# ConvFFN of a hybrid MLA/GLA layer on one core: the prompt's output gate folded into w_down, sums begun from the residual rows, gate and conv rows loaded at other places

## The chip, the cores and the metric

The kernel runs on one core of a Trainium2 chip. The metric is the device time of one launch in microseconds, as the median of several runs; less is better. The engines are named as the profile names them: PE (TensorE; PEld is its weight load), DVE (VectorE), ACT (ScalarE), POOL (GpSimd) and SP (SyncE, the queue that issues every transfer of this kernel).

## What is computed

One layer of a streaming encoder for a prompt of 2048 tokens and a sample of 64 tokens, all in float32, with 1024 model columns. The first half (projections, attention, gated linear attention) isn't touched by the change. The second half is, per sequence:

```
x  = x + mods[2][:, None, :] * mixed              # residual rows, the first gate
h  = _modulate(x, p['g_norm2'], mods[3], mods[4])
a, g = jnp.split(h @ p['w_up'], 2, axis=-1)       # 1024 -> 2 x 2816
a_ext = concat([hist, a]);  conv = b_conv + sum_j w_conv[j] * a_ext[:, j:j+L]    # width 3
f  = (gelu(conv) * g) @ p['w_down']               # 2816 -> 1024
y  = x + mods[5][:, None, :] * f                  # the second gate: one value per column and sequence
```

The last line can be written, for one sequence, as `y = x + u @ (w_down * gate)`, because the gate depends on the output column alone.

## The kernel before

**Products.** Every large product is made of three float32r products of a high and a low part: a `split` makes the high part on ACT (a cast) and the low part (source minus high part) on DVE or POOL. w_up is applied with a Strassen-like scheme of seven products of blocks (`PRODUCTS`), so each step also has block sums (POOL, line 1205), weight splits (ACT line 1456, DVE and POOL line 1398) and recombinations.

**Projection stage** (lines 1069 to 1137 and 1229 to 1254). `out_tile` is a generator, run for 17 tiles of tokens (16 of the prompt, one of the sample) with the steps load, mT, proj, res, norm and done interleaved by hand in the loop of line 1230. It multiplies by w_out, applies the first gate (line 1093), adds x and stores the residual rows in DRAM (`x1_d`, line 1096), normalises, and writes blocks for the up-projection: those of pass 0 stay on the chip (`h2`), those of the later passes go to DRAM (`comb_d`, lines 1134 to 1136). The gate row comes by `gate_rows` (line 1178), a broadcast to all partitions, once for the prompt (t = 0) and once for the sample (t = 16), into one buffer (`gate`, bufs=1 in that tag). `conv_rows` (line 1212) loads w_conv, b_conv and the sample's history as rows into the buffers `xn` and `comb`, which every tile also uses, and transposes them on PE to columns; it is called at t = 3.

**ConvFFN** (from line 1257). Three passes over the 22 blocks of 128 FFN columns, 66 steps: pass 0 and pass 1 have 6 tiles of the prompt each, pass 2 has the last 4 and the sample. Pass 1 goes through the blocks backwards, so the w_down rows of the last step of a pass serve the first step of the next (`wd_kept`). The function `slot(n, ...)` writes down the instructions of step n as events with times: `base` is the step's start, `end[m]` the end of product m, `after` the end of the step. The events are sorted by these times, and PE, ACT, DVE and POOL execute them in that order; only the transfers on SP are placed by the framework's own scheduler. In a step PE does products 1, 6, 2, 5, then down tiles (`"d"`) of the step before between products 3, 7, 4 and behind them:

```
seq = [1, 6, 2, 5, "d", 3, "d", 7, "d", 4] + ["d"] * 8
```

A down tile (`down_tile`, line 1485) is six matmuls into two PSUM banks (line 1496), and an addition of the two halves to the tile's sum `acc` on DVE (line 1507); in the first step of a pass the sum begins with a copy on ACT (line 1505). `rows` loads 128 rows of w_down (`sd`, line 1188), `rows_hi` and `lo` split them (ACT line 1433, DVE line 1398). In the last step of a pass each finished sum gets, in halves of 512 columns, a multiplication by the gate on DVE (`gate_`, line 1543), an addition of the residual rows on POOL (`finish_`, line 1548; the rows come as `xs`, line 1534, in two buffers) and a store (line 1549). For passes 0 and 1 these events are spread over the next step and a half by `late`; in pass 2 they follow the sums at once. The last step also fetches the inputs of the next pass (`fetch`, line 1480, 14 transfers of 768 KB). Eight `acc` buffers go round; three lie in the pool `ac0`, five in `ac1`, which is opened in place of the projection stage's `wk4b`. `conv_state` (line 1568) stores the convolution's last rows in the last step: two transposes, two copies on DVE to `ob`, two stores; `ob` takes the two buffers of `xs`.

Of the kernel before, what the change touches and what calls it, by code (L numbers as in the profile page):

```python
# [11 lines left out]
F32 = mybir.dt.float32  # L12
# [9 lines left out]
P = 128  # L22
# [39 lines left out]
def kernel(  # L62
# [1006 lines left out]
    def out_tile(t, n, seq, src, pos0, tok0):  # L1069
# [2 lines left out]
        yield "load"  # L1072
        wk = wk4
        if t in (0, NT):
            gt[seq] = gate_rows(wk, 0, seq, "gate")
        x = wk4b.tile([P, D], F32, tag="x", name="x", bufs=2)
        Q.dma_start(x[:n], src)
        mT = [wk.tile([P, KD, P], F32R, tag=f"mT{i}", name=f"mT{i}", bufs=2) for i in range(2)]
# [102 lines left out]

    c7 = ctx.enter_context(ExitStack())
    fw = None
    g2 = []

    def load_rows(f):
        s = fw.tile([P, D], F32, tag="fst", name="fst", bufs=4)
# [24 lines left out]
    def conv_rows(pool):  # L1212
        fr = pool.tile([4 * NF, P], F32, tag="xn", name="fr")
        Q.dma_start(fr[:3 * NF], w_conv.rearrange("j (f p) -> (j f) p", p=P))
        Q.dma_start(fr[3 * NF:], b_conv.rearrange("j (f p) -> (j f) p", p=P))
        fh = pool.tile([4 * NF, P], F32, tag="comb", name="fh")
        Q.dma_start(fh[:2 * NF], state_ffn_conv.rearrange("j (f p) -> (j f) p", p=P))
        for src, dst, n in ((fr, fcol, 4 * NF), (fh, hist, 2 * NF)):
            pt = bank()
            T.transpose(pt[:, :n], src[:n], ident[:n, :n])  # L1220
            V.tensor_copy(dst.rearrange("p j f -> p (j f)"), pt[:, :n])

    c6, c6a = ctx.enter_context(ExitStack()), ctx.enter_context(ExitStack())
    wk4b = c6.enter_context(tc.tile_pool(name="wk4b", bufs=1, side="right", reuse_waits="tile"))
# [1 line left out]

    next(outs[0])
    for t in range(len(tiles) - 1):  # L1230
        g, nxt = outs[t], outs[t + 1]
        last = t == len(tiles) - 2
        next(nxt)
        next(g)
        if t == 3:
            conv_rows(wk4b)
        if last:
            next(outs[t - 1])
            next(outs[t - 1])
            next(nxt)  # L1240
            next(nxt)
            project(t, t + 1, ks=range(3))
            next(outs[t - 1])
            project(t, t + 1, ks=range(3, KD))
        else:
            project(t)
            if t:
                next(outs[t - 1])
                next(outs[t - 1])
            next(nxt)  # L1250
            if t:
                next(outs[t - 1])
# [13 lines left out]
    with ExitStack() as c8:  # L1266
# [8 lines left out]
        def acc_tile():  # L1275

            nonlocal n_acc
            i, n_acc = n_acc % 8, n_acc + 1
            return ac[i > 2].tile([P, D], F32, tag=f"acc{i}", name="acc")

        halo = wk.tile([P, NF, 2], F32, tag="halo", name="halo")
        cout = [wk.tile([P, 2, NF], F32, tag=f"cout{s}", name=f"cout{s}") for s in range(2)]

# [21 lines left out]
        def slot(n, base, w, raw, raw_next, behind):  # L1305
# [121 lines left out]
            def rows():  # L1427
                o["sd"] = load_rows(f)

            def rows_hi():  # L1430
                nonlocal wd_kept
                o["wd"] = wd_kept = two("wd", (P, D))
                S.copy(o["wd"][0], o["sd"])  # L1433
# [1 line left out]
            def rows_kept():  # L1435
                o["wd"] = wd_kept

            if first_f and n:
                at(base + 2, rows_kept)
            else:  # L1440
                at(base + 2, rows)
                at(after + 1.0, rows_hi)
                at(after + 2.5, lambda: lo(o["wd"], o["sd"], V))

# [40 lines left out]
            def down_tile(i, t):  # L1485

                rows_ = P if i < nt else SMP
                c0 = i * P if i < nt else nt * P + 2

                def products():  # L1490
                    if first_f:
                        acc[i] = acc_tile()
                    o["po", i] = po = [bank(), bank()]
                    for a, b in ((0, 0), (0, 1), (1, 0)):
                        for c in range(2):
                            T.matmul(po[c][:rows_], o["u"][a][:, c0:c0 + rows_],  # L1496
                                     o["wd"][b][:, c * 512:(c + 1) * 512], start=a + b == 0, stop=a == 1)

                def add():
                    o["acc", i] = acc[i]  # L1500
                    for c in range(2):
                        cc = slice(c * 512, (c + 1) * 512)
                        x, y = acc[i][:rows_, cc], o["po", i][c][:rows_]
                        if first_f:
                            S.copy(x, y)
                        else:
                            V.tensor_tensor(x, x, y, op=ALU.add)  # L1507

                if n == 0 and i == 3:
                    at(t - .01, open_acc)  # L1510
                at(t, products)
                t += 6 * .232
                at(t + .1, add)
                if last_f:
                    tile_ = t0 + i if i < nt else NT
                    last = n + 1 == len(steps)
                    late = o.setdefault("late", t) + 5.5 * i + 1.6

                    def gate_load():
                        if i in (0, nt) and (n + 1 == NF or i == nt):  # L1520
                            if i == nt:
                                g2[:] = [acc_tile()]
                            else:
                                g2[:] = [ac[1].tile([P, D], F32, tag="gate", name="gate")]
                            Q.dma_start(g2[0], gate_d[1, int(i == nt):int(i == nt) + 1].partition_broadcast(P))
                        o["gate", i] = g2[0]

                    def residual(c):
                        if c == 0 or not last:
                            gate_load()  # L1530
                        src = x1_d[tile_ * P:tile_ * P + rows_]
                        if not last:
                            o["xs", i, c] = x = ac[1].tile([P, 512], F32, tag="xs", name="xs", bufs=2)
                            Q.dma_start(x[:rows_], src[:, c * 512:(c + 1) * 512])
                        elif c == 0:
                            x = fw.tile([P, D], F32, tag="fst", name="fst", bufs=4) if i < 3 else acc_tile()
                            Q.dma_start(x[:rows_], src)
                            o["xs", i, 0], o["xs", i, 1] = x[:, :512], x[:, 512:]

                    def gate_(c):  # L1540
                        cc = slice(c * 512, (c + 1) * 512)
# [3 lines left out]
                    def finish_(c):  # L1545
                        cc = slice(c * 512, (c + 1) * 512)
                        a = o["acc", i][:rows_, cc]
                        (V if last and i == nt and c else G).tensor_tensor(a, a, o["xs", i, c][:rows_], op=ALU.add)  # L1548
                        Q.dma_start((y_sample if i == nt else y_prompt[tile_ * P:tile_ * P + rows_])[:, cc], a)

                    for c in range(2):
                        at(base + 8.0 + i if last else late - 4 + c, residual, c)
                        at(t + 1.4 + c * .1 if last else late + 2.5 * c, gate_, c)
                        at(t + 1.5 + c * .1 if last else late + 1 + 2.5 * c, finish_, c)
                return t

            return after, w_next, [lambda t, i=i: down_tile(i, t) for i in range(nt + smp)]
# [10 lines left out]
        def conv_state():  # L1568
            for s, dst in ((0, conv_prompt), (1, conv_sample)):
                pt = bank()  # L1570
                T.transpose(pt[:2 * NF, :P], cout[s].rearrange("p j f -> p (j f)"), ident)
                ob = ac[1].tile([P, 512], F32, tag="xs", name="ob", bufs=2)
                V.tensor_copy(ob[:2 * NF, :P], pt[:2 * NF, :P])
                Q.dma_start(dst.rearrange("j (f p) -> (j f) p", p=P), ob[:2 * NF, :P])

# [78 lines left out]
```

## Time and profile before

| | us |
|---|---|
| median of 3 runs | 3186.03 (3184.51 to 3191.58) |
| the profiled execution | 3196.8 |
| its span, first to last instruction | 3195.0 |
| PE busy, DVE busy, POOL busy in the span | 3037.7, 2471.9, 1438.8 |
| the projection stage | about 1446 to 1683 |
| ConvFFN, pass 0, pass 1, pass 2 begin | 1683, 2232, 2751 |

Times in the views are microseconds from the span's start, durations of single instructions nanoseconds where "mean" or "median" is said. "PE bank L1326 x48" in the chain is a run of 48 matmuls of line 1326. A bracket at the end of a timeline row is the idle time of the engine before it and what ended it. A row of the table by stretches gives the stretch, its length, the busy time of PE, PEld, DVE, ACT and POOL with the number of instructions of each, PE's granted clock as a share of full speed, the busy share of the DMA engines and the GB/s moved. An "SPq" row is an issue of a transfer.

### The profile page before, as it was taken

Reading aid. Unit: us, or ns where it says so; the run is one execution under the profiler, and the core shown is the slowest. Engines: PE = TensorE matmul, PEld = TensorE weight load, DVE = VectorE, ACT = ScalarE, POOL = GpSimd, SP = SyncE. Lnnn points to the kernel's source line nnn. Section 1 sums busy time; section 2 is a strip of 40 time slices with the busy share of each in tenths; the row PEclk is TensorE's granted clock in tenths of the full one; section 3 lists DMA queues with packets and bytes.
Section 4 is the critical chain, followed back from the end, with each engine's and each line's share of the span. In section 5 each row is a group of like instructions: output and inputs, shape, how many; then the busy total and the mean of one; then the engine's idle time right before and its main releaser. Section 6 shows DMA issues by size and latency. Waiting matters only on the chain.

```text
span 3195.0 us, 46983 instructions
## 1 busy us (share of the span) xinstructions
PE 3037.7 (95%) x16730; PEld 2662.0 (83%) x16730; DVE 2471.9 (77%) x4642; ACT 1497.6 (47%) x3254; POOL 1438.8 (45%) x1194
## 2 busy tenths in 40 slices
PE   7999899999989999998995999999999999999997
PEld 4999788788758888886874999999899999889996
DVE  4776678778688888874564778777878787899998
ACT  4655433333257777773544443433444343344442
POOL 0223222212132222201446666664866666688885
PEclk9999899999979999999997999999999999999999
DMA  7554521111121112103474222224421212532322
GB/s 255 158 132 122 151 70 60 53 50 53 37 82 51 50 48 64 38 28 110 161 235 141 72 73 67 71 68 168 156 72 60 80 60 75 201 116 82 97 80 83
DMA packets 186778, 306.09 MB, mean 96 GB/s; under 512 B 59959, under 2 KB 112775, under 8 KB 186543
## 3 DMA queue, kind: packets, MB, share of 16 engines
q1 hardware_dynamic: 186543, 303.09, 30.2%
q8 instruction: 132, 2.16, 0.3%
q14 instruction: 103, 0.84, 0.1%
HBM read 227.79 MB, written 75.24 MB: 95 GB/s over the span
## 4 chain that ended last, share of the span: by engine, by line
PE 48%; POOL 4%; DVE 2%; DMA 2%; issue 1%; ACT 1%; POOLq 0%; DVEq 0%; SPq 0%
PE bank L1326 27%; PE bank L1496 15%; PE bank L96 3%; DMA comb_d<-comb 1%; PE bank L882 1%; PE bank L869 1%; POOL sraw L1205 1%; POOL comb L91 1%; DVE acc L1543 1%; DVE acc L1507 1%; POOL acc L1548 0%; ACT comb L1117 0%; POOL wu L1398 0%; PE bank L841 0%; PE bank L843 0%
## 5 line engine op out<-in xcount | busy, mean ns | idle before, releaser
L1326 PE MATMUL bank<-h,wu 128*128 128x384 f32 (+1 forms) x5544 | 958.1, 328 | 41.5 <-ACT m L1345 23.3
L1326 PEld LDWEIGHTS bank<-h,wu 128*128 128x128 f32 x5544 | 923.5, 190 | 71.4 <-ACT m L1345 27.5
L1496 PE MATMUL bank<-wd,u 128*128 128x512 f32 (+1 forms) x2244 | 567.7, 396 | 3.0 <-ACT wd L1433 1.4
L1398 POOL TENSOR_TENSOR wu<-sraw,wu 128x512 fp32r<-128x512 f32 x252 | 364.0, 1444 | 367.4 <-ACT wu L1456 367.2
L1507 DVE TENSOR_TENSOR acc<-acc,bank 128x512 f32<-128x512 f32 (+1 forms) x714 | 450.8, 678 | 48.5 <-PE bank L1496 45.5
L1496 PEld LDWEIGHTS bank<-wd,u 128*128 128x128 f32 (+1 forms) x2244 | 410.0, 186 | 87.4 <-ACT wd L1433 1.9
L96 PE MATMUL bank<-w_g,hs 128*128 128x512 f32 (+4 forms) x1632 | 319.6, 347 | 0.0
L1398 DVE TENSOR_TENSOR wu<-fst,wu 128x512 fp32r<-128x512 f32 x189 | 212.2, 1148 | 102.5 <-ACT wu L1456 100.9
L96 PEld LDWEIGHTS bank<-w_g,hs 128*128 128x128 f32 (+1 forms) x1632 | 249.8, 188 | 33.4 <-issue 2.7
L91 DVE TENSOR_TENSOR pp<-bank,pp 128x512 fp32r<-128x512 f32 (+5 forms) x344 | 196.2, 577 | 40.5 <-ACT pp L88 36.1
L882 PE MATMUL bank<-pp,vv 128*128 128x512 f32 (+5 forms) x688 | 210.8, 393 | 13.0 <-DVE ob L906 6.7
L857 ACT ACTIVATE pr<-bank,mx 128x512 f32<-128x512 f32 (+4 forms) x328 | 204.7, 629 | 30.6 <-DVE mx L850 21.1
L1384 DVE SCALAR_TENSOR_TENSOR cv<-a_sb,fcol,cv 128x768 f32<-128x768 f32 (+1 forms) x132 | 215.7, 1634 | 4.1 <-ACT cv L1380 1.8
L88 ACT CAST pp<-bank 128x512 fp32r<-128x512 f32 (+5 forms) x344 | 170.0, 504 | 103.5 <-PE bank L869 101.4
L845 DVE TENSOR_REDUCE mx<-bank 128x1 f32<-128x512 f32 (+4 forms) x328 | 195.0, 599 | 24.8 <-PE bank L844 18.8
L1351 POOL TENSOR_TENSOR m<-m,m 128x384 f32<-128x384 f32 (+1 forms) x132 | 172.8, 1309 | 72.9 <-ACT m L1345 66.8
L96 PE MATMUL bank<-w_o,mT 128*128 128x512 f32 (+1 forms) x816 | 199.1, 402 | 0.2 <-ACT mT L88 0.2
L1456 ACT CAST wu<-sraw 128x512 fp32r<-128x512 f32 x252 | 154.9, 615 | 78.5 <-PE bank L1326 49.0
L869 PE MATMUL bank<-ident,pr 128*128 128x128 f32 (+1 forms) x1112 | 181.0, 278 | 3.2 <-DVE pp L91 2.3
L1205 POOL TENSOR_TENSOR sraw<-fst 128x512 f32<-128x512 f32 x128 | 178.2, 1393 | 11.6 <-DMA fst<-w_up 11.6
L96 PEld LDWEIGHTS bank<-w_o,mT 128*128 128x128 f32 (+1 forms) x816 | 151.1, 188 | 38.9 <-ACT mT L88 0.5
L1345 ACT COPY m<-bank 128x384 f32<-128x384 f32 (+1 forms) x198 | 89.7, 453 | 172.1 <-PE bank L1326 170.9
(260 smaller groups left out, 5224.2 us busy)
## 6 DMA issues: line engine op xcount, KB each, us to landing
fst<-w_up SPq DMA_DIRECT2D x128, 512.0 KB
fst<-w_down SPq DMA_DIRECT2D x64, 512.0 KB
x<-x_prompt SPq DMA_DIRECT2D x32, 512.0 KB
ada_w<-w_ada SPq DMA_DIRECT2D x64, 256.0 KB
h<-comb_d SPq DMA_DIRECT2D x14, 768.0 KB
comb_d<-hi SPq DMA_DIRECT2D x10, 896.0 KB
wst<-w_ada SPq DMA_DIRECT2D x16, 512.0 KB
hT_d<-hT SPq DMA_DIRECT2D x16, 512.0 KB
```

Of the source, the lines that this page charges most:

```text
L91: (lo_eng or V).tensor_tensor(lo, src, hi.bitcast(F32), op=ALU.subtract)
L96: T.matmul(out, a, b, start=first and i == 0, stop=last and i == 2)
L845: V.reduce_max(mx[:qn, c:c + 1], po[:qn, :b - a], axis=AX.X)
L857: S.activation(pr[:qn, :b - a], box["s", i, j][:qn, :b - a], AF.Exp, bias=nb, accum_out=ls[:qn, i, j:j + 1])
L869: T.transpose(pt[:kn, i * qn:(i + 1) * qn], pr[:qn, j * P - a:j * P - a + kn], ident[:qn, :qn])
L882: T.matmul(box["o"][:, cs_], vv[:kn, key0 // P + j, :], pp[i][:kn, cs_], start=j == 0 and i == 0, stop=j == nk - 1 and i == 1)
L1205: G.tensor_tensor(s, x, y, op=op)
L1326: T.matmul(b, w[m][i][:, k], hv[j][:, :, k], start=first and k + i + j == 0, stop=k == 3 and i == 1, skip_group_check=not first)
L1384: V.scalar_tensor_tensor(v, o["a"][:, j:j + tot], col(j), v, op0=ALU.mult, op1=ALU.add)
L1398: eng.tensor_tensor(out[1], src, out[0].bitcast(F32), op=ALU.subtract)
L1496: T.matmul(po[c][:rows_], o["u"][a][:, c0:c0 + rows_], o["wd"][b][:, c * 512:(c + 1) * 512], start=a + b == 0, stop=a == 1)
L1507: V.tensor_tensor(x, x, y, op=ALU.add)
```

## The change

Four things. (a) In passes 0 and 1 each block of w_down rows is multiplied by the prompt's gate (`rows_gated`, 128 x 1024 on DVE, 43 times: not in step 22, which keeps the rows of step 21); step 44, the first of pass 2, loads its rows anew, without the gate. (b) In these passes the sum's buffer is loaded with the residual rows (`open_sum`) and every step adds to it on DVE; the finished sum is stored as it is, in one transfer. (c) The second gate's row is loaded once before the steps (`gate2`), so that two `acc` buffers remain in `ac0`; `ob` has a buffer of its own, one for both uses; the first gate of the sample goes into a buffer of `mx`. (d) `conv_rows` is a generator: its loads stand before the projection loop, its transposes behind the first tile's product.

```diff
         if t in (0, NT):
-            gt[seq] = gate_rows(wk, 0, seq, "gate")
+            gt[seq] = gate_rows(wk, 0, seq, "gate") if t == 0 else gate_rows(w3, 0, seq, "mx", 2)
...
         Q.dma_start(fh[:2 * NF], state_ffn_conv.rearrange("j (f p) -> (j f) p", p=P))
+        yield
         for src, dst, n in ((fr, fcol, 4 * NF), (fh, hist, 2 * NF)):
             pt = bank()
             T.transpose(pt[:, :n], src[:n], ident[:n, :n])
             V.tensor_copy(dst.rearrange("p j f -> p (j f)"), pt[:, :n])
+        yield
...
+    conv = conv_rows(wk4b)
+    next(conv)
     next(outs[0])
     for t in range(len(tiles) - 1):
...
-        if t == 3:
-            conv_rows(wk4b)
...
             project(t)
-            if t:
+            if t == 0:
+                next(conv)
+            else:
                 next(outs[t - 1])
                 next(outs[t - 1])
...
-            return ac[i > 2].tile([P, D], F32, tag=f"acc{i}", name="acc")
+            return ac[i > 1].tile([P, D], F32, tag=f"acc{i}", name="acc")
+
+        gate2 = gate_rows(wk, 1, 0, "gate2")
...
+            def rows_gated():
+                V.tensor_tensor(o["sd"], o["sd"], gate2, op=ALU.mult)
...
-            if first_f and n:
+            if n == NF:
                 at(base + 2, rows_kept)
             else:
                 at(base + 2, rows)
+                if p + 1 < len(PASSES):
+                    at(end[2] + .7, rows_gated)
                 at(after + 1.0, rows_hi)
                 at(after + 2.5, lambda: lo(o["wd"], o["sd"], V))
...
+                folded = p + 1 < len(PASSES)
+
+                def open_sum():
+                    acc[i] = acc_tile()
+                    if folded:
+                        Q.dma_start(acc[i], x1_d[(t0 + i) * P:(t0 + i + 1) * P])
+
                 def products():
-                    if first_f:
-                        acc[i] = acc_tile()
                     o["po", i] = po = [bank(), bank()]
...
-                        if first_f:
+                        if first_f and not folded:
                             S.copy(x, y)
                         else:
                             V.tensor_tensor(x, x, y, op=ALU.add)
 
-                if n == 0 and i == 3:
-                    at(t - .01, open_acc)
+                if first_f:
+                    if n == 0 and i == 0:
+                        at(27.5, open_acc)
+                    at(max(28.0 + .2 * i, t - 5.0) if folded else t, open_sum)
                 at(t, products)
...
-                if last_f:
...
+                if last_f and folded:
+                    at(t + 1.8, lambda: Q.dma_start(y_prompt[tile_ * P:tile_ * P + rows_], acc[i][:rows_]))
+                elif last_f:
 
                     def gate_load():
...
+                        o["gate", i] = gate2
+                        if i == nt:
+                            o["gate", i] = acc_tile()
+                            Q.dma_start(o["gate", i], gate_d[1, 1:2].partition_broadcast(P))
...
-                        at(base + 8.0 + i if last else late - 4 + c, residual, c)
-                        at(t + 1.4 + c * .1 if last else late + 2.5 * c, gate_, c)
-                        at(t + 1.5 + c * .1 if last else late + 1 + 2.5 * c, finish_, c)
+                        at(t + 1.4 + c * .1, gate_, c)
+                        at(t + 1.5 + c * .1, finish_, c)
...
-                ob = ac[1].tile([P, 512], F32, tag="xs", name="ob", bufs=2)
+                ob = ac[1].tile([P, P], F32, tag="ob", name="ob")
```

## Rows read from the trace of the kernel before

**Rows 1.** The page's first line.
```profile
span 3195.0 us, 46983 instructions
```

**Rows 2.** The table by stretches: two projections, a step of pass 1, two steps of pass 2.
```profile
1496.93:1510.60 13.67, 13.67 (x51) 10.87 (x51) 0.88 (x2) 0.00 (x0) 0.00 (x0) 0.82 0.00 0
...
1525.34:1536.58 11.24, 11.24 (x50) 9.01 (x50) 5.57 (x12) 6.24 (x14) 6.07 (x8) 1.00 0.24 93
...
2770.44:2821.23 50.79, 41.69 (x230) 36.34 (x230) 46.41 (x55) 20.82 (x42) 49.18 (x36) 0.90 0.53 171
2379.67:2402.87 23.20, 23.20 (x122) 21.57 (x121) 18.53 (x26) 9.32 (x16) 14.35 (x12) 1.00 0.24 69
```

**Rows 3.** The chain that ended last, in the ConvFFN: start, us, what.
```profile
2231.72 8.45 PE bank L1326 x48
...
2310.10 8.45 PE bank L1326 x48
...
2821.23 6.47 PE bank L1326 x48
...
2839.51 6.46 PE bank L1326 x48
```

**Rows 4.** Timeline of PE around the transposes of the conv rows.
```profile
1487.20 0.27 PE L1220 MATMUL bank<-ident,fr 88*128 88x88 f32 x1 [1.94 <-DMA fr<-b_conv]
1496.60 0.33 PE L1220 MATMUL bank<-ident,fh 44*128 44x44 f32 x1 [9.13 <-DMA fh<-state_ffn_conv]
```

**Rows 5.** Waits of the SP queue, 1672 to 1690: for whom, us in total, times, longest.
```profile
SPq L1178 <- DVE bank L1093: 10.6, 1, 10.6
```

**Rows 6.** Timeline of SP: the issue of the last three of four first w_up loads.
```profile
1688.15 3.85 SPq L1193 DMA_DIRECT2D fst<-w_up  x3
```

**Rows 7.** Timeline of POOL at the start of pass 0.
```profile
1695.73 1.26 POOL L1205 TENSOR_TENSOR sraw<-fst 128x512 f32<-128x512 f32 x1 [11.64 <-DMA fst<-w_up]
```

**Rows 8.** Instructions of lines 1543 and 1548: min/median/max ns, first and last start.
```profile
L1543 DVE TENSOR_TENSOR acc<-acc,gate x32: 673/1320/1784, 2242.6 to 3185.4; 128x512 f32<-128x512 f32 x32
...
L1548 POOL TENSOR_TENSOR acc<-acc,xs x24: 1285/1708/2005, 2243.3 to 2807.1; 128x512 f32<-128x512 f32 x24
```

**Rows 9.** Groups of DVE by form in 17 steps of pass 1: busy, mean ns, idle before.
```profile
L1398 DVE TENSOR_TENSOR wd<-fst,wd 128x1024 fp32r<-128x1024 f32 x17 | 20.8, 1221 | 0.0
```

**Rows 10.** Timeline of DVE: one busy moment behind pass 0, then a step of pass 1.
```profile
2289.34 2.30 DVE L1398 TENSOR_TENSOR wd<-fst,wd 128x1024 fp32r<-128x1024 f32 x1
...
2363.88 1.78 DVE L1398 TENSOR_TENSOR wu<-fst,wu 128x512 fp32r<-128x512 f32 x1 [2.46 <-ACT wu L1456]
2366.13 1.28 DVE L1507 TENSOR_TENSOR acc<-acc,bank 128x512 f32<-128x512 f32 x2 [0.47 <-PE bank L1496]
2368.53 0.56 DVE L1368 TENSOR_TENSOR a_sb<-m,bank 128x384 f32<-128x384 f32 x1 [1.11 <-issue]
...
2369.65 1.29 DVE L1507 TENSOR_TENSOR acc<-acc,bank 128x512 f32<-128x512 f32 x2 [0.35 <-PE bank L1496]
...
2375.66 0.54 DVE L1348 TENSOR_TENSOR m<-m,bank 128x384 f32<-128x384 f32 x1
```

**Rows 11.** Timeline of SP in the same step.
```profile
2359.68 0.33 SPq L1188 DMA_DIRECT2D fst<-w_down  x1
```

**Rows 12.** The transfer view, 2359 to 2369 in 40 slices: GB/s moved in each.
```profile
GB/s 0 0 0 0 0 0 131 131 98 229 197 393 410 311 213 279 229 344 426 262 279 131 131 0 0 0 0 0 0 0 98 262 213 246 197 360 426 180 115 0
```

**Rows 13.** Timeline of PE: three down tiles at the end of that step.
```profile
2375.30 4.38 PE L1496 MATMUL bank<-wd,u 128*128 128x512 f32 x18
```

**Rows 14.** The chain, 1474 to 1541: a small load from its issue to its landing.
```profile
1485.66 1.41 DMA fr<-b_conv
```

**Rows 15.** Timeline of DVE in the last step.
```profile
3164.17 0.48 DVE L1573 COPY ob<-bank 44x128 f32<-44x128 f32 x2 [1.33 <-PE bank L1571]
...
3170.62 1.21 DVE L1398 TENSOR_TENSOR wd<-fst,wd 128x1024 fp32r<-128x1024 f32 x1
```

**Rows 16.** Timeline of PE: the last down tiles.
```profile
3171.88 6.81 PE L1496 MATMUL bank<-wd,u 128*128 128x512 f32 x28 [1.12 <-DVE wd L1398]
```

More of the change, by code (lines that the diff above doesn't have):

```diff
@@ L1183 @@
     fw = None
-    g2 = []
     def load_rows(f):
@@ L1513, in down_tile, with residual @@
                 at(t + .1, add)
-                if last_f:
-                    tile_ = t0 + i if i < nt else NT
-                    last = n + 1 == len(steps)
-                    late = o.setdefault("late", t) + 5.5 * i + 1.6
+                tile_ = t0 + i if i < nt else NT
+                if last_f and folded:
+                    at(t + 1.8, lambda: Q.dma_start(y_prompt[tile_ * P:tile_ * P + rows_], acc[i][:rows_]))
+                elif last_f:
                     def gate_load():
[L1520 to L1538, printed above, removed]
+                        o["gate", i] = gate2
+                        if i == nt:
+                            o["gate", i] = acc_tile()
+                            Q.dma_start(o["gate", i], gate_d[1, 1:2].partition_broadcast(P))
+                    def residual():
+                        gate_load()
+                        x = o["xs", i] = fw.tile([P, D], F32, tag="fst", name="fst", bufs=4) if i < 3 else acc_tile()
+                        Q.dma_start(x[:rows_], x1_d[tile_ * P:tile_ * P + rows_])
                     def gate_(c):
@@ L1547, in finish_ @@
                         a = o["acc", i][:rows_, cc]
-                        (V if last and i == nt and c else G).tensor_tensor(a, a, o["xs", i, c][:rows_], op=ALU.add)
+                        (V if i == nt and c else G).tensor_tensor(a, a, o["xs", i][:rows_, cc], op=ALU.add)
                         Q.dma_start((y_sample if i == nt else y_prompt[tile_ * P:tile_ * P + rows_])[:, cc], a)
+                    at(base + 8.0 + i, residual)
                     for c in range(2):
-                        at(base + 8.0 + i if last else late - 4 + c, residual, c)
-                        at(t + 1.4 + c * .1 if last else late + 2.5 * c, gate_, c)
-                        at(t + 1.5 + c * .1 if last else late + 1 + 2.5 * c, finish_, c)
+                        at(t + 1.4 + c * .1, gate_, c)
+                        at(t + 1.5 + c * .1, finish_, c)
                 return t
@@ L1571, in conv_state @@
                 T.transpose(pt[:2 * NF, :P], cout[s].rearrange("p j f -> p (j f)"), ident)
-                ob = ac[1].tile([P, 512], F32, tag="xs", name="ob", bufs=2)
+                ob = ac[1].tile([P, P], F32, tag="ob", name="ob", bufs=2)
                 V.tensor_copy(ob[:2 * NF, :P], pt[:2 * NF, :P])
```

## Prediction

> **What bounds the kernel now.** The profiled execution took 3196.8 us with a span of 3195.0 [rows 1]; the sum below is made against it, and the median of the runs, 3186.0, is 10.8 us less, so I take differences alone over to the median. First I read the table by stretches. A step of passes 0 and 1 takes 23.20 us, and PE is busy for all of it; DVE works 18.53 us of it, POOL 14.35 [rows 2]. In steady steps PE is the bound, and nothing that this change moves between DVE, ACT and POOL can shorten one. It can win only where PE waits, and lose where it makes PE wait. So I went through the chain for places in which the steps are not regular, and found four that the diff touches.
>
> The first is the conv rows in the projection stage: PE idles 1.94 and then 9.13 us for their loads [rows 4], and the 48 matmuls behind take 13.67 us at a granted clock of 0.82 (between 1.2 and 2.4 GHz), where the same work takes 11.24 at 1.00 later [rows 2]. The second is the start of pass 0: SP stands 10.6 us behind one load, the sample's first gate, which needs the buffer that DVE's last multiplication of the prompt reads [rows 5]; w_up loads wait behind it until 1688.15 [rows 6], and POOL starves 11.64 us for them [rows 7]. The third and fourth are the two pass boundaries. The three steps from 2231.72 to 2310.10 [rows 3] take 78.38 us; three regular ones would take 69.60, so 8.8 are lost. Behind pass 1, 50.79 us pass where two regular steps stand [rows 2], 36.56 by the period of 18.28 in pass 2 [rows 3], so 14.2 are lost. In the latter stretch POOL is busy 49.18 of 50.79 us and DVE 46.41 [rows 2]: the gate's multiplications (median 1.32 us, up to 1.78) and the residual additions (median 1.71) [rows 8] hold up the recombinations that free PE's banks.
>
> **The parts and their price.**
>
> *Conv rows.* The loads are issued ahead of the first tile's product (48 matmuls, 11.24 us [rows 2]) and the transposes stand behind it, where 1.41 us is what one load takes [rows 14]. The two transposes (0.27 and 0.33 us [rows 4]) and two small copies stay, at another tile. Gone are 1.94 + 9.13 = 11.1 us of idle PE, and 13.67 - 11.24 = 2.4 of slow clock: 13.5. Low end 11.1, if the clock is still recovering from something else. On SP three small issues, some 0.33 us each [rows 11], pass the first tile's gate and x, which are read behind that product too. The buffers `xn` and `comb` are free of conv rows before the first tile's norm needs them. The stage behind is bound by PE too, so the gain is not taken back.
>
> *The sample's gate.* Its buffer is free as soon as tile 15 is transposed, so the wait of 10.6 us goes. What is late next on SP: the stores of tile 14's blocks and of tile 15's residual rows, which stand in front of three of the four w_up loads and wait for DVE's work on the same tiles. If the scheduler leaves them there, the loads come earlier by the gate's own issue, about 1.3 us (three took 3.85 [rows 6]); if it puts the loads ahead, POOL's 11.6 us [rows 7] go. The order on SP isn't written in the code. I take the lower, 1.3, since nothing but the gate is taken out of the order, and keep 0 and 11.6 as ends.
>
> *The multiplications into w_down.* 43 of 128 x 1024. The nearest row is the subtraction of the same shape on DVE, 1.22 us [rows 9], 2.30 with POOL at work beside it [rows 10]: 52 to 99 us of DVE in all. DVE idles 23.20 - 18.53 = 4.7 us a step, so there is room, but the multiplication has its place: behind the addition of product 6, at 2361.42 in the step shown (the 2.46 us of idle ahead of 2363.88 [rows 10]). Its rows are issued at 2359.68 [rows 11]; with the w_up rows behind them they land between 2362.8 (half of the 1.05 MB moved) and 2364.9 (all of it) [rows 12]. It ends between 2362.8 + 1.22 = 2364.0 and 2364.9 + 2.30 = 2367.2. Queued behind it is the split of product 2's block, 0.69 to 1.78 us, which ended at 2365.66; at worst it ends at 2369.0, 3.3 us late. Behind that come idle times of 0.47, 1.11 and 0.35 us [rows 10], which take up 1.9: DVE goes into the taps at most 1.4 us late. Who waits for DVE there is PE's last down tile, which needs the bank that the addition at 2375.66 (+0.54 = 2376.20) frees [rows 10] and starts at 2375.30 + 2 x 1.40 = 2378.1 [rows 13]: 1.9 us of slack. Price: nothing at either end, by 0.5 us at the worse one. POOL has 8.8 us of idle a step.
>
> *The boundary behind pass 0.* Gone: 12 gate multiplications (12 x 1.32 = 16 us of DVE), 12 additions (12 x 1.71 = 21 us of POOL), 12 half loads with two buffers on SP, 12 copies on ACT. Added: 12 additions on DVE at about 0.64 [rows 10], 8 us, as in any step, and 6 loads of whole residual tiles. The boundary steps then hold a regular step's work, and I take all of the 8.8 us. Low end 0: the loads wait for the stores of the buffers that they reuse, and SP stands still in front of w_up. The loads of the next pass's inputs aren't the cause now, since PE ran the step from 2231.72 without a pause, so they need not become one.
>
> *The boundary behind pass 1.* The same 12 and 12 go, nothing comes on DVE but one more split of w_down rows (1.22 to 2.30 us), with a cast on ACT and a load in step 44. Of 14.2 us I take 13, low end 5 (a third).
>
> *The start of pass 0* has the 12 additions in place of copies on ACT, and six loads. The sums for the tiles 2 to 5 lie where the projection's last tile is stored from, so these loads wait for that store, and the first additions for them. Price 0, for a whole step of PE's work lies between; at worst one load's landing, 2.6 us (half of 5.2 for two [rows 11, 12]).
>
> *The last step.* `ob` has one buffer for two uses: DVE's second copy now waits for the first store, where both took 0.48 us together [rows 15]. Behind it stand the second tap, the last split of w_down (3170.62 [rows 15]) for which PE's last matmuls wait [rows 16], and then DVE's own additions and gates to the end. A small transfer takes 1.41 us [rows 14], with 0.33 for the issue [rows 11] 1.7 us, and all of it is on the path. The ends are 0, if something else on DVE has to wait as long there, and 5.2, which two loads of 512 KB took [rows 11, 12]. The Trainium skill (DMA: Bandwidth & Descriptors, "Anatomy of one DMA") gives about 2.0 us as the fixed cost of a transfer, on another issuing path; with it this term would be 2.3 and the sum 0.6 smaller. The trace has 1.41 for a load and no store of this kind with somebody waiting.
>
> Sum: 13.5 + 1.3 + 8.8 + 13 - 1.7 = 34.9 us less: 3186.0 - 34.9 = 3151. The lows make 11.1 + 0 + 0 + 5 - 2.6 - 5.2 = 8 (3178), the highs 13.5 + 11.6 + 8.8 + 14.2 = 48 (3138).
>
> **The rivals.**
>
> *The w_up loads come 10 us earlier.* For it: they need only memory that the projection's weights leave, and the first of the four was issued before the gate. Against it: the other three were not ahead of the stores in the order before. Time: 3151 - 10 = 3141. 14%.
>
> *The boundaries keep their pauses.* SP is in order, and a load of residual rows into a buffer whose store hasn't landed stops w_up and w_down behind it; before, SP waited there too, for POOL, and PE's waits were put down to ACT and POOL. If half of the 21.8 us stay and the start loses a little: about 3165 to 3170. 14%.
>
> *Slower: the multiplication stops DVE, and DVE stops PE, in each of 43 steps.* It is the only new wait of a regular step: a load's landing now stands in the middle of DVE's queue, where before nobody read it until the next step. For it: 0.5 us between my worst case and the slack. Against it: DVE's 4.7 us of idle. It cancels the rest at 34.9 / 43 = 0.81 us a step, and is slower by 0.2% (6.4 us) at 0.96; for that the rows would have to land at about 2366.4 or later with POOL beside the multiplication, some 6.7 us behind the issue. At 1.1 us a step: 3198. 6% for that, and 6% for the stretch between, where nothing can be told from no change. The skill (SBUF: State Buffer, "Who interferes with whom") says that DVE with two SBUF inputs and a reading POOL instruction exclude each other for a whole instruction; the trace agrees in kind, 1.22 against 2.30, and it would hold POOL back as well, which speaks for this rival.
>
> **How the numbers follow.** The forecast has 60%: 3151, with its own range from 3146 to 3160. Early loads 14% (3141), kept pauses 14% (3168), cancelled 6% (3180 to 3192), slower 6%. About 0.2% is what a measurement of this kernel can tell from no change: its three runs lie 7 us apart. Faster 0.88, same 0.06, slower 0.06. The range from 3139 to 3173 leaves out the last two cases and a little of each side.
>
> **What would show it.** PE without idle at line 1220 and 48 matmuls in 11.2 us behind; steps of 23.2 us in passes 0 and 1, with the multiplication ending before 2367 in a step that begins as the one shown; both boundaries within 2 us of regular steps, no lines 1543 and 1548 there; about 1.5 us between the two copies to `ob`. It is wrong if a regular step is longer than 23.3 us, if PE waits at the boundaries for banks or w_up still, or if the start of pass 0 changes by more than 5 us.

## The result, and the profile after

| | before | after |
|---|---|---|
| median of 4 runs, us | 3185.27 (3183.45 to 3191.58) | 3151.76 (3147.85 to 3157.83) |
| ratio after / before | | 0.9891, 95% interval 0.9873 to 0.9908 |
| profiled execution, us | 3196.8 | 3147.85 |
| its span, us | 3195.0 | 3146.0 |
| from TensorE's first projection product to the end of the span, us | 1748.1 | 1713.95 |

The change makes the kernel 33.5 us faster. The two spans differ by 49.0 us, but 14.8 of that lie ahead of the first projection product, where the two programs are the same: executions of one program differ there by several us (the changed kernel's first projection begins at 1432.05 in this trace and at 1437.25 in that of after_again below). So traces are compared below by the last row of the table, from that product on, or by shorter stretches.

**The conv rows.** Timeline of PE (start, us, engine, line, operation, tiles; in brackets the idle time before it), against [rows 4]:

```profile
1432.05 11.51 PE L96 MATMUL bank<-w_o,mT 128*128 128x512 f32 x48 [0.24 <-ACT mT L88]
1443.40 0.24 PE L1220 MATMUL bank<-ident,fr 88*128 88x88 f32 x1
1443.57 0.26 PE L1220 MATMUL bank<-ident,fh 44*128 44x44 f32 x1
...
1630.38 9.77 PE L96 MATMUL bank<-w_o,mT 128*128 128x512 f32 x40 [1.16 <-DVE x L1094]
...
1640.77 13.26 PE L96 MATMUL bank<-w_o,mT 128*128 128x512 f32 x56
...
1678.00 8.90 PE L1331 MATMUL bank<-h,wu 128*128 128x384 f32 x34 [4.04 <-POOL wu L91]
1690.15 6.04 PE L1331 MATMUL bank<-h,wu 128*128 128x384 f32 x24 [3.25 <-ACT m L1350]
...
1720.85 6.28 PE L1331 MATMUL bank<-h,wu 128*128 128x384 f32 x24 [4.25 <-ACT m L1350]
```

The same view of the kernel before: the first and the last product of the stage, and the 24 products at which the opening below ends.

```profile
1446.89 1.19 PE L96 MATMUL bank<-w_o,mT 128*128 128x512 f32 x4 [0.24 <-ACT mT L88]
...
1667.46 13.70 PE L96 MATMUL bank<-w_o,mT 128*128 128x512 f32 x58
...
1746.71 6.41 PE L1326 MATMUL bank<-h,wu 128*128 128x384 f32 x24 [4.96 <-ACT m L1345]
```

No bracket stands behind the two transposes: the rows are there when PE comes to them. The projection stage, from 1432.05 to 1640.77 + 13.26 = 1654.03, takes 222.0 us; before it took from 1446.89 to 1667.46 + 13.70 = 1681.16, 234.3. That is 12.3 us. By the table by stretches PE's busy time in the stage fell from 222.4 to 219.8 us, so the 2.6 us of slow clock went, and its idle time from 11.9 to 2.2: the 11.1 us are gone, and 1.4 are new, most of them the wait of 1.16 us for DVE at 1630.38.

**The start of pass 0.** From 1654.03 to the 24 products at 1720.85 pass 66.8 us; before, 65.55 (1681.16 to 1746.71). This stretch, the opening below, lost 1.3 us. Timeline of SP in it, against [rows 6]:

```profile
1654.06 0.33 SPq L1505 DMA_DIRECT2D acc<-x_d  x1
1654.95 0.36 SPq L1134 DMA_DIRECT2D comb_d<-hi  x1
1655.36 0.55 SPq L1505 DMA_DIRECT2D acc<-x_d  x1
...
1658.67 1.71 SPq L1192 DMA_DIRECT2D fst<-w_up  x1
...
1661.92 2.79 SPq L1192 DMA_DIRECT2D fst<-w_up  x2
...
1665.65 0.58 SPq L1192 DMA_DIRECT2D fst<-w_up  x1
```

And SP's waits from 1652 to 1680, against [rows 5] (for whom, us in total, times, longest):

```profile
SPq L1505 <- PE bank L96: 9.8, 1, 9.8
```

The wait of 10.6 us for the sample's gate is gone, and one of 9.8 has its place: the first residual load goes into memory that the last projection still reads. POOL starves 13.56 us for w_up, where it was 11.64 [rows 7]:

```profile
1669.60 1.29 POOL L1204 TENSOR_TENSOR sraw<-fst 128x512 f32<-128x512 f32 x1 [13.56 <-DMA fst<-w_up]
```

**The boundaries.** The chain that ended last (start, us, what), against [rows 3]:

```profile
2205.72 8.45 PE bank L1331 x48
...
2275.30 8.45 PE bank L1331 x48
...
2715.97 6.46 PE bank L1331 x48
2735.64 6.47 PE bank L1331 x48
...
2772.20 6.46 PE bank L1331 x48
```

The three steps from 2205.72 take 69.58 us, 23.19 each, through the first boundary, and the two from 2735.64 take 36.56, 18.28 each, behind the second. (The first step of pass 2 takes 19.67, as it did before: it still does six down tiles, the later ones five.) The table by stretches for a regular step of pass 1 and two steps behind pass 1 (length, then busy us and instructions of PE, its loads, DVE, ACT, POOL; clock, DMA share, GB/s), against [rows 2]:

```profile
2344.88:2368.07 23.19, 23.19 (x121) 21.57 (x121) 20.15 (x27) 9.31 (x16) 15.74 (x12) 1.00 0.22 69
2735.64:2772.20 36.56, 36.56 (x231) 33.29 (x230) 29.57 (x46) 22.06 (x43) 27.53 (x23) 1.00 0.51 166
```

The two steps that took 50.79 us take 36.56, with POOL busy 27.53 us in place of 49.18. All 8.8 and 14.2 us are gained.

**The multiplication.** Timeline of DVE in a step of pass 1, against [rows 10]:

```profile
2328.54 1.61 DVE L1436 TENSOR_TENSOR fst<-fst,gate 128x1024 f32<-128x1024 f32 x1 [1.91 <-DMA fst<-w_down]
2330.08 1.78 DVE L1403 TENSOR_TENSOR wu<-fst,wu 128x512 fp32r<-128x512 f32 x1
2331.78 1.27 DVE L1522 TENSOR_TENSOR acc<-acc,bank 128x512 f32<-128x512 f32 x2
2333.74 0.56 DVE L1373 TENSOR_TENSOR a_sb<-m,bank 128x384 f32<-128x384 f32 x1 [0.68 <-issue]
...
2334.85 1.29 DVE L1522 TENSOR_TENSOR acc<-acc,bank 128x512 f32<-128x512 f32 x2 [0.35 <-PE bank L1511]
```

DVE now waits 1.91 us for the rows where it used to wait 2.46 for a cast of ACT's; the step keeps its length.

**The last step.** Timeline of DVE, against [rows 15]:

```profile
3115.12 0.48 DVE L1580 COPY ob<-bank 44x128 f32<-44x128 f32 x2 [1.33 <-PE bank L1578]
```

Both copies still take 0.48 us together; nothing waits between them. The `+` line of the change ends in `name="ob", bufs=2)`: `ob` has two buffers of its own. The diff above lacks these last words, and the text above it is wrong with "one for both uses".

The parts sum to 12.3 - 1.3 + 8.8 + 14.2 + 0 = 34.0 us; the medians say 33.5.

### The profile page after: what moved, and what is told of

It reads as the page before. It is cut to its first block, busy times and chain, and to the rows that moved or that the text cites. A ratio compares the mean times of both kernels' runs of the same rounds, so it can differ in the third digit from the quotient of the medians.

```text
span 3146.0 us, 46900 instructions
## 1 busy us (share of the span) xinstructions
PE 3014.4 (96%) x16730; PEld 2645.2 (84%) x16730; DVE 2502.1 (80%) x4686; ACT 1486.7 (47%) x3231; POOL 1452.6 (46%) x1170
## 4 chain that ended last, share of the span: by engine, by line
PE 51%; POOL 2%; DVE 2%; DMA 2%; ACT 1%; issue 1%; SPq 0%; DVEq 0%; POOLq 0%; ACTq 0%
PE bank L1331 28%; PE bank L1511 16%; PE bank L96 3%; DMA comb_d<-comb 1%; PE bank L882 1%; PE bank L869 1%; POOL comb L91 1%; PE bank L841 0%; PE bank L843 0%; ACT comb L1117 0%; DVE acc L1550 0%; PE bank L844 0%; DVE comb L1119 0%; DVE acc L1522 0%; POOL comb L1122 0%
## 5 line engine op out<-in xcount | busy, mean ns | idle before, releaser
L1403 POOL TENSOR_TENSOR wu<-sraw,wu 128x512 fp32r<-128x512 f32 x252 | 382.5, 1518 | 337.5 <-ACT wu L1466 333.1
L1522 DVE TENSOR_TENSOR acc<-acc,bank 128x512 f32<-128x512 f32 (+1 forms) x738 | 464.8, 677 | 29.4 <-PE bank L1511 26.5
```

Source lines behind the costliest of these rows:

```text
L1403: eng.tensor_tensor(out[1], src, out[0].bitcast(F32), op=ALU.subtract)
```

## The experiments

Times are medians, ratios are to the kernel before on the same chip. The first three experiments ran on one chip (kernel before: 3189.98 us, 9 runs), together with the changed kernel itself, **after_again**:

> The changed kernel itself beside the others on one chip, as their measure: 3152 us, ratio 0.989; in its trace the projection stage 222.0 us, the opening of pass 0 66.8 us.

It took 3156.17 us (ratio 0.9888, 0.9874 to 0.9903), with an opening of 66.7 us: 3151.8 on one chip is 3156 on this one.

**1. The conv rows alone.** Only the two `yield`s of `conv_rows` and the calls that go with them are put into the kernel before:

```diff
+    conv = conv_rows(wk4b)
+    next(conv)
     next(outs[0])
...
-        if t == 3:
-            conv_rows(wk4b)
...
-            if t:
+            if t == 0:
+                next(conv)
+            else:
```

> The kernel before with the change's fourth part alone: the conv and gate rows (fr, fh) are loaded ahead of the first projection and transposed behind it, nothing else is changed. Theory: of the change's gain in the projection stage (234.3 us before, 222.0 us in the changed kernel) all comes from this part, since TensorE no longer waits 11.1 us for fr and no longer restarts at the lower clock; the stage takes 222 to 223 us, and the kernel 3173 us (12.3 us less than 3185, ratio 0.9961). Rival: the projection ends earlier, but the ConvFFN's first products wait for w_up rows that the queue can bring no earlier, so the opening takes back what the stage gave, and the time stays within 3 us of 3185 (ratio over 0.999).

Measured: 3179.61 us, ratio 0.9956 (0.9942 to 0.9971), 10.4 us less; from the first product on 1736.3 us, 11.8 less. Timeline of PE:

```profile
1437.59 11.51 PE L96 MATMUL bank<-w_o,mT 128*128 128x512 f32 x48 [0.24 <-ACT mT L88]
1448.94 0.24 PE L1221 MATMUL bank<-ident,fr 88*128 88x88 f32 x1
...
1636.35 11.26 PE L96 MATMUL bank<-w_o,mT 128*128 128x512 f32 x40 [1.68 <-DVE x L1094]
```

The idle time is gone and the opening, 64.7 us, takes nothing back, so the rival falls. The stage takes 223.9 us, a little over what was expected: behind a wait of 1.68 us 40 products took 11.26 us here, at a granted clock of 0.85. In after_again, with the same wait (1.69), they took 9.75 at 1.00. With one trace of each it stays open whether these 1.5 us belong to the program or to the execution. The wait itself is in all ten traces with the early conv rows, 1.1 to 1.7 us long, and in none of the three without; its cause wasn't looked for.

**2. The opening: the residual loads behind w_up (loads_first).**

```diff
-        gate2 = gate_rows(wk, 1, 0, "gate2")
+        with tc.issue_after(loads[3].ins):
+            gate2 = gate_rows(wk, 1, 0, "gate2")
...
                     if folded:
+                      with tc.issue_after(loads[3].ins):
                         Q.dma_start(acc[i], x1_d[...])
```

> The changed kernel, with the loads of the residual rows into the sums of pass 0 (and the gate rows) put behind the first four w_up loads in SP's queue; same work. Theory: the 1.3 us that the opening of pass 0 lost come from the residual loads, which wait 9.8 us on SP for the projection's last products with the w_up loads behind them; with w_up ahead, the stretch from the projection's end to the first block of 24 up products falls from 66.8 to 63 to 65 us, and the kernel from 3151.8 to 3149 us (ratio to the kernel before 0.988). Rival: the opening is bound by something else (POOL's block sums behind the last tiles' norm), the stretch stays 66 to 67 us and the time 3152.

Measured: 3156.41 us, 0.9882 (0.9862 to 0.9902); opening 66.45. My theory fell. SP's waits there, 1650 to 1680:

```profile
SPq L1134 <- ACT hi L88: 14.3, 2, 10.9
```

Without the residual load in front, the next in the queue, the store of the 15th tile's blocks, waits about as long (10.9 us) for ACT's cast of its data. The removed wait of 10.6 us before and the new one of 9.8 both covered this one.

**3. All four w_up loads ahead of those stores (loads_ahead).** As loads_first, and the 15th tile's three stores get an ordering edge behind the four loads, which also have a higher priority in the scheduler:

```diff
+    for x in stores_of[tiles[-3][0]]:
+        for y in loads:
+            tc.add_manual_dep(x.ins, y.ins.name, ...)
```

> As loads_first, and the four w_up loads are put ahead of the 15th tile's three stores too, so that SP reaches them while TensorE is in the last projection (their memory is that of w_o's first rows, which are read early in it); same work. Theory: SP's queue is what holds the opening: the first w_up load is issued at or before the projection's end rather than 4.6 us behind it, the opening falls by 6 to 11 us from 66.8, and the kernel takes 3141 to 3146 us (ratio 0.986 to 0.988). Rival: behind the loads stands the splitting on ScalarE, VectorE and POOL, which are busy with the last tiles' norm until some 10 us behind the projection; the opening gains no more than in loads_first, 3 us at most, and the time is 3149 or more.

Measured: 3146.67 us, 0.9858 (0.9844 to 0.9872), 9.5 us below after_again: a kernel faster than both. Timeline of SP, of PE, then of POOL:

```profile
1649.33 3.77 SPq L1197 DMA_DIRECT2D fst<-w_up  x4
```

```profile
1645.86 13.26 PE L96 MATMUL bank<-w_o,mT 128*128 128x512 f32 x56
...
1715.75 6.32 PE L1341 MATMUL bank<-h,wu 128*128 128x384 f32 x24 [4.25 <-ACT m L1360]
```

```profile
1662.06 1.44 POOL L1209 TENSOR_TENSOR sraw<-fst 128x512 f32<-128x512 f32 x1
```

The opening takes 56.6 us, so the theory holds (the time lies 0.7 us over its range) and the rival falls. The loads are issued 9.8 us ahead of the projection's end, and POOL begins its block sums as soon as it is done with the tile's norm, with no wait for w_up.

**4. One load ahead (one_load_ahead)**: the inner loop of experiment 3 over `loads[:1]`. 

> As loads_first, but of the four w_up loads the first alone is put ahead of the 15th tile's three stores; in the kernel before it stood there too (issued 9.7 us before the projection's end, against 4.6 us behind it in the changed kernel). Theory: that this one load moved behind the stores is the whole loss of the opening, so it falls from 66.5 us in loads_first to between 64 and 65.6, what it was with the load ahead (64.7 in conv_alone, 65.6 before); the time is 1 to 2.5 us below that of loads_first. Rival: the block sums need all four loads, the first one early is worth nothing, and the opening stays at 66.4 us or more.

Measured on another chip: 3155.03 us where the kernel before took 3184.80, 0.9903 (0.9887 to 0.9920); opening 66.65. The theory fell here too. The openings in us behind the end of the projection, worked out from SP's, POOL's and PE's timelines; "34 products" is the block that waits for POOL's last product matrix:

| kernel | first w_up issued | second w_up issued | POOL's first block sum | 34 products start | next 24 take | opening |
|---|---|---|---|---|---|---|
| before | -9.7 | 7.0 | 14.6 | 22.9 | 6.03 | 65.55 |
| conv_alone | -10.3 | 6.35 | 13.7 | 22.05 | 5.98 | 64.7 |
| after | 4.6 | 7.9 | 15.6 | 24.0 | 6.04 | 66.8 |
| after_again | 5.5 | 8.3 | 15.5 | 23.8 | 6.03 | 66.7 |
| loads_first | 5.4 | 6.8 | 14.0 | 22.6 | 6.99 | 66.45 |
| one_load_ahead | -9.7 | 7.1 | 14.4 | 22.7 | 7.10 | 66.65 |
| loads_ahead | -9.8 | -8.4 | 2.9 | 12.5 | 6.52 | 56.6 |

The first load early is worth nothing (22.6 against 22.7). The rival's result came, but not for its reason: the block sums of the first step need two of the four loads (`block_sum(raws[0], m)`), and it is the second that sets the start: the chain that ended last goes from its issue (1688.15 in the kernel before [rows 6]) to POOL's first sum. In the six kernels whose POOL waits for w_up, its first sum begins 7.2 to 7.7 us behind the issue of the second load, and the 34 products 8.3 to 8.7 us behind that. In the changed kernel the second load comes 0.9 to 1.3 us later than before, since the residual loads are issued among the stores ahead of it, and the 34 products start 1.1 us later (24.0 against 22.9). That is 1.1 of the 1.3 us. Both kernels without that delay (loads_first, one_load_ahead) start 1.1 to 1.2 us earlier than after_again and lose 1.0 in the next 24 products, over which the granted clock is 0.60 and 0.59 in place of 0.72. Why it stays low there in both wasn't tried.

**5. The boundaries.** The kernel before without the gate (before_no_gate: `gate_` at the last pass only), and without POOL's addition (before_no_add):

```diff
-                        at(t + 1.4 + c * .1 if last else late + 2.5 * c, gate_, c)
+                        if last:
+                            at(t + 1.4 + c * .1, gate_, c)
```

```diff
-                        (V if last and i == nt and c else G).tensor_tensor(a, a, ...)
+                        if last:
+                            (V if i == nt and c else G).tensor_tensor(a, a, ...)
```

> The kernel before without the 24 multiplications by the second gate on VectorE in passes 0 and 1 (the prompt's ConvFFN rows of these passes stay ungated; loads and POOL's residual additions stay). Theory: the pauses at the boundaries (8.8 us behind pass 0, 14.2 behind pass 1) come from POOL, which is busy 49.2 of 50.8 us behind pass 1, so most of them stay: together 15 us or more of 23.0, and the kernel takes 3180 us or more. Rival: they come from VectorE, whose queue the multiplications lengthen by 16 us a boundary: both pauses fall under 3 us together, and the time falls by about 20, to 3169.

> The kernel before without the 24 additions of the residual rows on POOL in passes 0 and 1 (the residual is left out of these passes' rows; its loads and VectorE's multiplications stay). Theory (POOL): with 21 us of POOL's work gone from each boundary the pauses fall under 6 us together of 23.0, and the kernel takes 3172 us or less. Rival (VectorE): they stay, 15 us or more, and the time is 3182 or more. If each alone takes away about half, both engines' queues make the pause.

Measured: 3179.41 us without the gate (0.9968, 0.9955 to 0.9980), 3175.85 without the addition (0.9952, 0.9934 to 0.9971), where before took 3191.03. Timeline of PE behind pass 0 and behind pass 1, without the gate and then without the addition:

```profile
2244.42 8.61 PE L1326 MATMUL bank<-h,wu 128*128 128x384 f32 x48
...
2294.43 8.61 PE L1326 MATMUL bank<-h,wu 128*128 128x384 f32 x48
...
2754.78 6.63 PE L1326 MATMUL bank<-h,wu 128*128 128x288 f32 x48
...
2799.55 6.62 PE L1326 MATMUL bank<-h,wu 128*128 128x288 f32 x48
```

```profile
2240.90 8.61 PE L1326 MATMUL bank<-h,wu 128*128 128x384 f32 x48
...
2267.83 8.59 PE L1326 MATMUL bank<-h,wu 128*128 128x384 f32 x48
...
2750.68 6.63 PE L1326 MATMUL bank<-h,wu 128*128 128x288 f32 x48
...
2829.04 6.62 PE L1326 MATMUL bank<-h,wu 128*128 128x288 f32 x48
```

Behind pass 1, without the gate two steps take 44.77 us, 8.2 over 36.56; without the addition four take 78.36, 5.3 over 73.1. Behind pass 0 without the gate two steps take 50.01 us, 3.6 over 46.39; without the addition one takes 26.93, 3.8 over this execution's 23.16; before, 8.8 were lost there. So of 23.0 us 11.8 are left without the gate and 9.1 without the addition. Both theories and both rivals fall, and what the second expectation says last came: neither engine alone made the pauses. The gate's multiplications were worth 11.2 us, the additions 13.9, each about half, and the change, which takes both away, leaves none. A kernel without just these two wasn't run; the change also takes away the half loads in two buffers and the copies on ACT, and what those were worth isn't shown apart.

**6. The multiplication left out, twice, and three times.** From the changed kernel, `rows_gated` isn't placed (after_no_mult), or holds a loop:

```diff
-                V.tensor_tensor(o["sd"], o["sd"], gate2, op=ALU.mult)
+                for _ in range(2):
+                    V.tensor_tensor(o["sd"], o["sd"], gate2, op=ALU.mult)
```

> The changed kernel without the 43 multiplications of the gate into w_down's rows (the prompt's second gate is left out in passes 0 and 1). Theory: they lie in VectorE's idle time and cost nothing; regular steps stay 23.19 us, and the time is within 3 us of the changed kernel's (ratio to the kernel before 0.989, interval included 0.987 to 0.991). Rival: they slow the ends of some steps or POOL's recombinations behind the boundaries: 0.1 us a step would be 4 us, and the ratio 0.9875 or less.

> The changed kernel with the gate multiplied twice into w_down's rows in each of the 43 steps (the prompt's second gate comes in squared in passes 0 and 1). One more multiplication is 1.2 to 1.8 us; behind it VectorE idles 0.68 + 0.35 us in the step read, PE's last down tile leaves 1.9 us more, and VectorE's 20.15 busy us of 23.19 become some 21.8. Theory: this still fits, steps stay 23.2 us and the time is within 3 us of the changed kernel's. Rival: the slack is smaller than I read, what is beyond 1.0 us (0.2 to 0.8) goes into every step: 8 to 34 us longer than the changed kernel, ratio 0.992 to 1.000.

> The changed kernel with three multiplications in each of the 43 steps (the prompt's second gate comes in cubed in passes 0 and 1). With two, VectorE was busy 23.56 of a step's 23.77 us. Theory: from there on VectorE is the bound and the third multiplication goes into the step at its whole length, 1.2 to 2.1 us: steps of 25.0 to 25.9 us, the kernel 50 to 90 us longer than after_twice. Rival: with two it was still a wait of PE's for a bank that ScalarE, stopped by VectorE, had not emptied, with idle time of VectorE elsewhere to use: the third costs less than 1 us a step, under 43 us in all.

Measured: 3159.19 us without it (0.9902, 0.9886 to 0.9919), 3178.08 with two (0.9960, 0.9947 to 0.9973), 3229.42 with three (one run). Without it nothing is gained: from the first product on 1714.6 us, against 1713.95 with it. A second costs about 0.55 us a step (1737.6 - 1713.95 = 23.65 over 43), a third 1.16 more (1787.5 - 1737.6 = 49.9 over 43). Table by stretches with two, then with three:

```profile
2343.58:2367.35 23.77, 23.45 (x122) 21.46 (x120) 23.56 (x30) 9.20 (x16) 16.71 (x12) 1.00 0.22 67
```

```profile
2347.96:2372.98 25.02, 23.45 (x121) 21.48 (x120) 23.86 (x30) 9.19 (x16) 16.55 (x12) 1.00 0.21 64
```

With two, DVE is busy 23.56 of 23.77 us here (22.72 in the next step): one more instruction, 1.6 us by the median, added 2.6 to 3.4 us of busy time, since others got longer too (two splits of `wu` took 3.49 in place of 1.29). DVE has next to no room left, as the theory for three had it; the theory for two had missed it, and its rival had the size. How it reaches PE, by the timeline of ACT and then of PE, with two:

```profile
2358.95 1.03 ACT L1385 ACTIVATE cv<-a_sb,fcol 128x768 f32<-128x768 f32 x1 [5.73 <-DVE a_sb L1373]
...
2360.40 0.47 ACT L1350 COPY m<-bank 128x384 f32<-128x384 f32 x1
```

```profile
2360.92 2.38 PE L1331 MATMUL bank<-h,wu 128*128 128x384 f32 x12 [0.33 <-ACT m L1350]
```

ACT stands 5.73 us for DVE's `a_sb` (3.16 in the changed kernel), and the copy that empties PE's bank is queued behind; PE waits 0.33 us for it, where the changed kernel has no such wait. With three, PE waits 1.57 us at the same place, the step shown grows by 1.25 us more, at the low edge of what was expected, so its rival (under 1 us) falls, and DVE idles 0.91 us in it for the rows' landing.

**7. One buffer for `ob`.**

```diff
-                ob = ac[1].tile([P, P], F32, tag="ob", name="ob", bufs=2)
+                ob = ac[1].tile([P, P], F32, tag="ob", name="ob", bufs=1)
```

> The changed kernel with one buffer for the two rows of the last step's `ob` in place of two. Theory (the prediction's working for this term, with the premise made true): VectorE's second copy waits for the first store, some 1.7 us (1.5 to 5.2) lie between the two copies, the last split of w_down starts that much later, and the stretch from the copies to the end is 1.7 us longer. Rival: it is hidden, the split waits as long for ScalarE's cast of the same rows, and the stretch is the same within 0.3 us.

One run, 3155.17 us, too near to tell; the trace does. Timeline of DVE:

```profile
3119.99 0.28 DVE L1580 COPY ob<-bank 44x128 f32<-44x128 f32 x1 [1.33 <-PE bank L1578]
3121.75 0.28 DVE L1580 COPY ob<-bank 44x128 f32<-44x128 f32 x1 [1.48 <-PE bank L1331]
...
3127.93 1.21 DVE L1403 TENSOR_TENSOR wd<-fst,wd 128x1024 fp32r<-128x1024 f32 x1
```

The second copy waits 1.48 us. The row names PE, which was long done; the chain that ended last goes from the first copy through its store, 1.33 us from issue to landing, to the second:

```profile
3120.30 1.33 DMA conv_prompt<-ob
```

The split of w_down starts 7.94 us behind the first copy, against 6.45 in the changed kernel, 1.5 later; to the end it is 33.4 against 30.9 us, 2.5 later, as PE's last 28 products took 8.35 in place of 6.81, at a granted clock of 0.80 in place of 1.00. The theory holds, with the wait at its low edge, and the rival falls.

## Why the prediction held, point by point

The forecast was 3151 us, the result 3151.8, and its sum of 34.9 stands against 34.0. Two of its terms were wrong, by 2.6 and 1.7 us in opposite directions, and two more were off by 1.2 each, one way and the other, so part of this closeness is luck.

- *Conv rows, 13.5:* 12.3. The 11.1 us of idle went, as experiment 1 shows by itself, and so did the slow clock, 2.6 us of PE's busy time where 2.4 were forecast. "The gain is not taken back" failed by 1.4 us: PE now waits for DVE's `x` late in the stage (1.16 us here, 1.1 to 1.7 in every trace with the early rows).
- *The sample's gate, 1.3 gained:* 1.3 lost. The step that failed is "nothing but the gate is taken out of the order": the residual loads, priced at 0, came into SP's order there and put off the second w_up load, for which POOL waits, by 0.9 to 1.3 us. The prediction was right about what is late next on SP, the 15th tile's stores (loads_first: 10.9 us for ACT's cast), and that made the wait of 10.6 us worthless. The rival of the early loads, 10 us, wasn't what this order did; brought about by hand it gave 9.5.
- *The multiplications, 0:* shown by after_no_mult. The rows land some 3.7 us behind their issue (2324.88 to 2328.54; 3.1 to 5.2 were worked out), and the multiplication takes 1.61 in the median (1.22 to 2.30 were taken). But the slack was read at the wrong place: not PE's last down tile with 1.9 us, but ACT's queue behind `a_sb` is reached first, and a second multiplication already cost 0.55 us a step. The rival of a slower kernel needed rows that land 6.7 us behind the issue, 3 us later than they do; its mechanism, DVE stopping PE in every step, is real, as two and three multiplications show.
- *Boundary behind pass 0, 8.8, and behind pass 1, 13:* 8.8 and 14.2. The named cause, gate and additions together, holds: in experiment 5 neither without the other makes up the pause. The rival of kept pauses fell: SP's loads and stores are there, and PE doesn't wait.
- *The last step, -1.7:* 0. "`ob` has one buffer for two uses" was a misreading: the line of the kernel itself asks for two. With one, the wait is 1.48 us and costs 1.5 to 2.5. The working was right and its premise was not. The Trainium skill (DMA: Bandwidth & Descriptors, "Anatomy of one DMA") gives about 2.0 us as the fixed cost of a transfer that GpSimd issues; the store that SP issues here took 1.33 us from issue to landing, so that figure would have made the wait too long.

## What to carry to other kernels

A wait on an in-order queue is worth only what the next instruction behind it would not have waited anyway: before a wait is priced, look when the data of the next three in the queue are ready, and count what the change itself puts between them. Work folded into operands that are loaded anyway cost nothing here where its engine had 4.7 us of idle time in a step, and 0.55 us a step where it had 3.0 left: read the margin at the first engine that queues behind it, not at the last one. A tile's buffer count is on its own line: read it before pricing a wait.

## What the runs showed of the hardware that was not expected

The multiplication on DVE lengthens POOL's work beside it: POOL's block sum `sraw<-fst,sraw`, 64 times, took 1292 ns in the median before, 1295 in after_no_mult and 2280 in the changed kernel. It goes the other way as well: DVE's multiplication took 1218 ns at best, 1611 in the median, and 2199 in the median with two a step. With two, that block sum is back at 1296, and POOL's splits `wu<-sraw,wu` went from 1299 before to 1720 in the median; in the step shown with two, such a split lies beside the multiplications and takes 2.27 us. What gets longer is the instruction that runs at the same moment. Line view of the changed kernel (min/median/max ns, first and last start, forms), then of after_no_mult:

```profile
L1204 POOL TENSOR_TENSOR sraw<-fst,sraw x64: 1257/2280/2287, 1675.5 to 3090.6; 128x512 f32<-128x512 f32 x64
```

```profile
L1204 POOL TENSOR_TENSOR sraw<-fst,sraw x64: 1252/1295/1747, 1687.2 to 3103.0; 128x512 f32<-128x512 f32 x64
```

So here one instruction put into DVE's idle time made POOL busy 15.74 us in a step in place of 14.35 [rows 2], and the room left is smaller than the idle time says: 3.0 us of DVE were free in a step, and one more instruction of 1.6 us left 0.2 and 1.05 of them in the two steps read.
